# Prompt-key compression ahead of the state-space sums; stacking copies on ScalarE; low parts of K on VectorE

## The chip, the cores and the metric

The kernel runs on one core of one Trainium2 chip. TensorE (PE) multiplies, VectorE (DVE), ScalarE (ACT) and GpSimd (POOL) do the rest, and SyncE (SP) issues nearly all DMAs. The metric is device time in microseconds (us), as the median of several runs; a profile is one further execution, taken with the hardware profiler.

## The reference, cut to what matters

One layer of a hybrid decoder, for a prompt of 512 tokens and 8 single sample tokens (520 columns in all). A Mamba-2 branch and a sparse-attention branch read one normalised input; both are projected, merged and followed by a ConvFFN. The change touches the seam between the two branches:

```
y = _rmsnorm(y * silu(z), ssm_norm_w)            # end of the state-space branch
y_ssm @ w_ssm_out

def _compress(k, pe, w1, w2):                    # keys (and values) of the prompt, 32 tokens to one
    sub = k.reshape(b, nj, 16, N_KV_HEADS, 64)
    hid = einsum("ld,lde->e", pe, w1)
    for r in range(2):
        hid = hid + einsum("bjshd,sde->bjhe", sub, w1[r*16:(r+1)*16])[:, r:r+nc]
    return einsum("bnhe,ed->bnhd", silu(hid), w2)

scores = einsum("bqhgd,bkhd->bqhgk", q, k) * ATT_SCALE    # selected and window attention
```

The norm of the state-space branch needs the sum of squares over all 2048 channels of each token. The compression needs the first two K/V streams of all four KV heads. Attention of a head needs its K in two parts: a rounded high part and the low part, the rest, so that three cheap products stand for a float32 one.

## The kernel before, in words

Every weight matrix is read in tiles of 128x1024 floats (512 KB) by SP into one of two raw buffers, `wr`. ACT rounds each half to a high part `wh` (L310), and DVE or POOL subtracts it to give the low part `wl` (L315, in turn). A raw buffer is free for the next load when both of its halves are split. The weights w1k and w1v of the compression are used raw: their buffers are free only when TensorE has used them (`drop`). Loads are issued strictly in the order in which the program asks for the weights.

A dense tile (`dense`) is up to 8 steps of 6 matmuls into one of two PSUM buffers `d`; a third tile can start only when the first has been read out of its buffer.

`run` steps two generators, a main one and a side one. Each yields a cost; the side gets a step when the main's costs have paid for it. A planner (first pass) sets the ratio of the two. The instructions are then put in order, engine by engine, by a scheduler that works on this program order; each engine takes its instructions strictly in that order, and waits where one is not ready.

The stretch of the change is one such `run` in `emit`. Main: four tiles `cmp_tile(h)`, which project the keys and values of the compression, rotate the keys (`rope`: shuffle on DVE, product on POOL, product and sum on DVE), write them out, and stack even and odd tokens on two halves of the partitions by four copies into `KP` (named K in the profile, L1160 on DVE and L439 on ACT); then `y1(3)`, eight dense tiles of half length with the weights w_so, mixed with `pages`, 16 gathers by POOL (`P<-pool_kv`), each written back by SP (`dr_kv<-P`); then the projections of attention head 0. Side: `ssm_rstd`, which sums the squares (`s<-ones,SQ`), forms the reciprocal root and spreads it over the partitions (`s<-cst,V`); then `compress_p(0)`, 16 products with the stacked keys (`s<-K,wr`), a SiLU from a tanh on ACT, and products with w2k; then `compress_p(1)`, the same for the values. `ssm_rstd` begins by yielding RSA = 14000, so that it starts late, and has a second pause, RSC = 8000, before it spreads.

The attention heads are prepared in `head_in` (L1318 to L1328): ACT writes the high part of K twice, POOL and DVE subtract for one low part each, per branch.

Of the kernel before, what the change touches and what calls it, by code (L numbers as in the profile page):

```python
# [13 lines left out]
ALU = mybir.AluOpType  # L14
# [77 lines left out]
LEAD = 20  # L92
LEAD_B = 0
RSC = 8000.0
RSA = 14000.0
FC = 6
FLAG = 2
VLAG = 4
# [267 lines left out]
class Emit:  # L366
# [778 lines left out]
    def cmp_tile(self, h):  # L1145

        nc, pc = self.nc, self.pc
        d = yield from self.in_tile(("cmp", h))
        R = self.t(self.cp, "S2", [P, T], 4)
        self.act(R[64:128], d[64:128, OFF:OFF + T])  # L1150
        self.rope(d, 64, R)
        nc.sync.dma_start(self.A["o_kv"][3 * h], R)
        for j in range(2):
            src = R[64 * j:64 * j + 64, 0:SEQ].rearrange("p (n i s) -> p i n s", i=8, s=2)
            for s in range(2):
                dst = self.KP[64 * s:64 * s + 64, j, :, h, 0:32]
                if s == j:
                    self.act(dst, src[:, :, :, s])
                else:
                    nc.vector.tensor_copy(dst, src[:, :, :, s])  # L1160
        self.done.add(("cmp", h))

    def pages(self):
# [130 lines left out]
    def head_in(self, h):  # L1294

        nc, pc = self.nc, self.pc
        self.Q[h] = []
        for j in (2 * h, 2 * h + 1):
            d = yield from self.in_tile(("q", j))
            R = self.t(self.cp, "S2", [P, T], 4)  # L1300
            self.rope(d, P, R)
            for q in range(2):
                head = 2 * j + q
                Qs = self.t(pc, "Q", [P, SEQ], 8, F32R)
                a, b = slice(64 * q, 64 * q + 64), slice(64 * (1 - q), 64 * (1 - q) + 64)
                self.act(Qs[a], R[a, 0:SEQ], scale=0.125)
                self.stt(Qs[b], R[a, 0:SEQ], 0.125, Qs[a], ALU.mult, ALU.subtract)
                self.Q[h].append(Qs)
                hh = 64 * (h % 2)
                dst = self.qs[hh:hh + 64].rearrange("p a c x -> p (a c x)")  # L1310
                for par in range(2):
                    o = par * 256 + (h // 2) * P + par * 16 + head
                    self.ts(dst[:, o:o + 97:32], R[a, SEQ + par:T:2], 0.125, eng=nc.gpsimd)
        d = yield from self.in_tile(("k", h))
        R = self.t(self.cp, "S2", [P, T], 4)
        self.rope(d, P, R)
        nc.sync.dma_start(self.A["o_kv"][3 * h + 1], R)
        K = self.t(pc, "K", [P, 4, SEQ], 2, F32R)  # L1318
        self.K[h] = K
        for br in range(2):  # L1320
            a, b = slice(64 * br, 64 * br + 64), slice(64 * (1 - br), 64 * (1 - br) + 64)
            r = R[a, 0:SEQ]
            self.act(K[a, 2 * br], r)
            self.act(K[b, 2 * br], r)
            self.tt(K[a, 2 * br + 1], r, K[a, 2 * br], ALU.subtract, nc.gpsimd)
            self.tt(K[b, 2 * br + 1], r, K[a, 2 * br], ALU.subtract)
            hh = 64 * (h % 2)
            nc.gpsimd.tensor_copy(self.kn[hh:hh + 64, br, h // 2, :], R[a, SEQ:T])  # L1328
        d = yield from self.in_tile(("v", h))
        R = self.t(self.cp, "S2", [P, T], 4)  # L1330
        self.act(R, d[:, OFF:OFF + T])
        nc.sync.dma_start(self.A["o_kv"][3 * h + 2], R)
        yield 0.0
        pv = self.ps_s()
        for c in range(4):
            nc.tensor.transpose(pv[:, c * P:(c + 1) * P], R[:, c * P:(c + 1) * P], self.ident)
        V = self.t(pc, "V", [P, 4, P], 2)
        nc.vector.tensor_copy(V, pv.rearrange("p (c d) -> p c d", c=4))
        self.V[h] = V
        pn = self.ps_s()  # L1340
        nc.tensor.transpose(pn[0:NB, 0:P], R[:, SEQ:T], self.ident)
        nc.vector.tensor_copy(self.vn[:, :, h, :], pn[0:NB, 0:P].rearrange("p (a d) -> p a d", a=2))
        yield 500.0
        self.done.add(("head", h))
# [262 lines left out]
            self.act(self.G2[n], d[:, OFF:OFF + T], AF.Tanh, scale=0.5)  # L1607

    def ssm_rstd(self):
        yield RSA  # L1610
        for g in range(4):
            yield from self.need(("ssm", g))
        rb = []
        for part in range(2):
            lo, hi = self.span(part)
            d = self.ps_s()
            self.sums(d, self.SQ[:, lo:hi], True, True, part)
            rb.append(self.rstd5(d, 2048, self.pc, part, "V"))
        yield RSC
        self.rs = self.SQ  # L1620
        for part in range(2):
            lo, hi = self.span(part)
            self.act(self.rs[:, lo:hi], self.spread(rb[part], part))
        yield 1700.0
# [271 lines left out]
    def emit(self):  # L1896
        nc, tc, A = self.nc, self.tc, self.A
        self.X, self.BC, self.Z, self.Y, self.Q, self.K, self.V, self.F, self.HS = ({} for _ in range(9))

        def seq(*gens):  # L1900
            for g in gens:
                yield from g

        def ada(a, b):
            return seq(*[self.ada(nb) for nb in range(a, b)])
# [18 lines left out]
        with tc.tile_pool(name="cp", bufs=1) as self.cp, tc.tile_pool(name="ps", bufs=1, space=PSUM) as self.ps, \  # L1924
                tc.tile_pool(name="dr", bufs=1, space=DRAM) as self.dr:
            self.W = Weights(nc, self.cp, self.jobs(), self.order and self.order[1],
                             queue=lambda i: self.queue if i < 2 else nc.sync.dma_start)
            self.setup()
            self.phase_a()
            with tc.tile_pool(name="pb", bufs=1, reuse_waits="tile") as self.pb:  # L1930
                self.setup_b()
                self.done.add(("yfree", 0))

                def scan(g):
                    return mix(self.ssd(g), self.ssm_step(g))
                self.run(self.group_in(0), self.misc())
                self.run(seq(self.group_z(0), self.group_in(1)), scan(0), LEAD_B, PUSH)
                self.run(seq(self.group_z(1), self.y1(0), self.group_in(2)), scan(1), LEAD_B, PUSH)
                self.run(seq(self.group_z(2), self.y1(1), self.group_in(3)), scan(2), LEAD_B, PUSH)
                self.run(seq(self.group_z(3), self.y1(2)), scan(3), LEAD_B, 1.5)  # L1940
                nc.sync.dma_start(A["o_conv"], self.convo)
            with tc.tile_pool(name="mid2", bufs=1, reuse_waits="tile") as self.mid2:
                with tc.tile_pool(name="pc", bufs=1, reuse_waits="tile") as self.pc:
                    self.setup_c()
                    self.run(seq(*[self.cmp_tile(h) for h in range(4)], mix(self.y1(3), self.pages()), self.head_in(0)),
                             seq(self.ssm_rstd(), self.compress_p(0), self.compress_p(1)))
                    self.dump("Y1", self.Y1)
                    self.att_hi = self.t(self.cp, "S16", [P, KD, T], 4, F32R)
                    self.att_lo = self.t(self.mid2, "M16", [P, KD, T], 1, F32R)
                    for h in range(3):  # L1950
                        self.run(mix(seq(self.head_in(h + 1), self.gate1(range(2 * h, 2 * h + 2))),
                                     ada(8 + 3 * h, 11 + 3 * h)), self.attend(h), LEAD, PUSH_C)
                    self.run(mix(seq(self.gate1(range(6, 8)), self.gate2()), ada(17, 20)),
                             seq(self.attend(3), self.sample_attend()), LEAD, PUSH_C)
                    self.run(self.merge())
                with tc.tile_pool(name="pe", bufs=1, reuse_waits="tile") as self.pe:
                    self.W.extend(self.pe, 2, 1)
                    self.W.lo_engines = [nc.vector, nc.vector, nc.gpsimd]
                    self.x2 = self.t(self.pe, "x2", [P, KD, T])
                    nc.sync.dma_start(self.x2, A["xT"])  # L1960
                    self.run(self.out_proj())
                    self.dump("x2", self.x2)
                    with tc.tile_pool(name="pf", bufs=1, reuse_waits="tile") as self.pf:
                        self.setup_f()
                        for ci in range(len(F_CHUNKS)):
                            self.run(self.ffn_up(ci))
                            if ci == len(F_CHUNKS) - 1:
                                nc.sync.dma_start(A["o_ffn"], self.ffno)
                            self.run(self.ffn_down(ci))
# [30 lines left out]
```

## Time and profile before

| | us |
|---|---|
| median of 3 runs (lowest, highest) | 1459.07 (1458.52, 1460.3) |
| the profiled execution | 1463.65 |
| its span, first to last instruction | 1461.9 |

| engine | busy us | share of the span |
|---|---|---|
| PE | 1403.5 | 96% |
| DVE | 919.2 | 63% |
| ACT | 693.5 | 47% |
| POOL | 443.2 | 30% |

The busy time of PE is nearly the whole span, so that what the kernel can gain or lose is the time in which PE waits or runs at its lower clock. Times in the rows below are counted from the start of the span. In a timeline row the brackets hold the idle time just before the row's first instruction and what ended it.

### The profile page before, as it was taken

How to read it: one execution, taken by the hardware profiler on the slowest of the kernel's cores; microseconds unless marked ns; L12 is line 12 of the kernel's file. 1: busy time of each engine (PE TensorE's matmuls, PEld its weight loads, DVE VectorE, ACT ScalarE, POOL GpSimd, SP SyncE). 2: the span in 40 equal slices, each digit the busy share in tenths (PEclk: the TensorE clock that was granted, in tenths of full speed). 3: DMA queues.
4: the chain of work that ended last, by engine and by line, in shares of the span. 5: the costliest groups of instructions: out<-in, count | busy, mean ns of one | idle time of the engine just before them, and what ended most of it. 6: DMA issues, size and time to landing. Idle time of an engine off the chain costs nothing.

```text
span 1461.9 us, 28894 instructions
## 1 busy us (share of the span) xinstructions
PE 1403.5 (96%) x11407; PEld 1281.9 (88%) x11407; DVE 919.2 (63%) x1842; ACT 693.5 (47%) x1528; POOL 443.2 (30%) x466
## 2 busy tenths in 40 slices
PE   7999899999999899999999999999899999999996
PEld 5899698999898888887878787899799999999996
DVE  1678987688789657857577561244576636653653
ACT  2565656565664336636555462233454324432443
POOL 4113655355456644303122011121321111111114
PEclk8999999999999999999999999999999999999998
DMA  9646545355353574213131226326422234332221
GB/s 373 232 121 190 164 152 186 110 169 180 123 180 119 183 253 158 75 58 102 44 131 59 70 76 202 130 88 219 138 87 87 88 101 139 135 113 91 80 77 59
DMA packets 73672, 195.30 MB, mean 134 GB/s; under 512 B 8480, under 2 KB 21312, under 8 KB 73280
## 3 DMA queue, kind: packets, MB, share of 16 engines
q1 hardware_dynamic: 70272, 184.00, 38.1%
q0 software_dynamic: 2720, 8.92, 1.8%
q8 instruction: 90, 1.47, 0.4%
q10 hardware_dynamic: 544, 0.54, 0.1%
q14 instruction: 46, 0.38, 0.1%
HBM read 173.10 MB, written 24.49 MB: 135 GB/s over the span
## 4 chain that ended last, share of the span: by engine, by line
PE 79%; DVE 7%; DMA 6%; ACT 3%; issue 2%; POOL 2%; SPq 0%; DVEq 0%; ACTq 0%; POOLq 0%
PE d L391 62%; PE s L391 14%; PE s L1418 2%; DMA wr<-w_in 2%; DMA wr<-w_out 1%; ACT wh L310 1%; DVE wl L315 1%; DVE S L423 1%; DVE st L426 1%; POOL yd L423 1%; DMA S<-ada 1%; ACT S L439 1%; POOL sq L423 0%; POOL wl L315 0%; DMA csx<-dr_cs 0%
## 5 line engine op out<-in xcount | busy, mean ns | idle before, releaser
L391 PE MATMUL d<-S,wh 128*128 128x256 f32 (+1 forms) x4640 | 832.4, 290 | 27.1 <-DVE S L423 7.3
L391 PEld LDWEIGHTS d<-S,wh 128*128 128x128 f32 x4640 | 669.8, 191 | 56.2 <-issue 34.2
L391 PE MATMUL d<-S,wl 128*128 128x256 f32 (+1 forms) x2672 | 557.8, 286 | 1.0 <-DVE wl L315 1.0
L391 PEld LDWEIGHTS d<-S,wl 128*128 128x128 f32 x2672 | 422.8, 190 | 6.2 <-issue 4.5
L310 ACT ACTIVATE wh<-wr 128x512 fp32r<-128x512 f32 (+1 forms) x354 | 217.1, 622 | 386.4 <-PE d L391 305.9
L315 POOL TENSOR_TENSOR wl<-wr,wh 128x512 fp32r<-128x512 f32 (+1 forms) x147 | 196.3, 1336 | 611.4 <-ACT wh L310 556.9
L315 DVE TENSOR_TENSOR wl<-wr,wh 128x512 fp32r<-128x512 f32 x207 | 155.4, 753 | 122.7 <-ACT wh L310 110.6
L391 PE MATMUL d<-M,wh 128*128 128x256 f32 (+1 forms) x960 | 197.1, 284 | 0.9 <-DVE M L423 0.7
L391 PEld LDWEIGHTS d<-M,wh 128*128 128x128 f32 x960 | 149.7, 188 | 1.5 <-DVE M L423 0.9
L439 ACT ACTIVATE P<-s,sm 128x256 f32<-128x256 f32 (+3 forms) x128 | 66.7, 524 | 65.1 <-DVE sm L1400 61.0
L1400 DVE TENSOR_REDUCE sm<-s 128x1 f32<-128x512 f32 (+3 forms) x96 | 57.1, 596 | 33.0 <-PE s L391 32.3
L426 DVE SCALAR_TENSOR_TENSOR S<-d,fww,S 128x511 f32<-128x511 f32 x84 | 62.9, 749 | 14.4 <-ACT S L439 14.4
L439 ACT ACTIVATE PT<-s 128x512 f32<-128x512 f32 (+2 forms) x96 | 49.8, 523 | 39.8 <-PE s L1418 39.7
L439 ACT ACTIVATE S<-S 128x520 f32<-128x520 f32 (+4 forms) x83 | 49.3, 598 | 40.5 <-DVE S L423 16.9
L423 DVE TENSOR_TENSOR S<-S,S 128x520 f32<-128x520 f32 (+2 forms) x66 | 45.1, 683 | 35.5 <-ACT S L439 33.9
L391 PE MATMUL s<-PT,V 128*64 128x128 f32 x640 | 64.3, 286 | 0.0
L391 PE MATMUL s<-K,Q 128*128 128x256 f32 (+3 forms) x256 | 60.2, 337 | 1.8 <-ACT PT L439 1.6
L431 DVE TENSOR_SCALAR P<-P,sm,gates 128x256 f32<-128x256 f32 (+3 forms) x128 | 59.9, 489 | 2.4
L439 ACT ACTIVATE so<-bcb,xd 128x128 f32<-128x128 f32 x128 | 41.0, 391 | 40.9 <-DVE ys L1105 27.6
L426 DVE SCALAR_TENSOR_TENSOR st<-st,dts,so 128x128 f32<-128x128 f32 x128 | 54.1, 469 | 7.0 <-ACT so L439 7.0
L426 DVE SCALAR_TENSOR_TENSOR S<-d,cwh,S 128x511 f32<-128x511 f32 (+2 forms) x72 | 53.4, 741 | 1.2 <-ACT S L439 0.8
L426 DVE SCALAR_TENSOR_TENSOR x<-d,mod,x 128x512 f32<-128x512 f32 (+1 forms) x26 | 18.4, 710 | 55.2 <-PE d L391 55.1
(311 smaller groups left out, 1700.1 us busy)
## 6 DMA issues: line engine op xcount, KB each, us to landing
wr<-w_in SPq DMA_DIRECT2D x77, 512.0 KB
wr<-w_up SPq DMA_DIRECT2D x44, 512.0 KB
wr<-ada SPq DMA_DIRECT2D x40, 512.0 KB
st<-sst SPq DMA_DIRECT2D x32, 256.0 KB
csb<-dr_cs SPq DMA_DIRECT2D x16, 512.0 KB
o_ssms<-st SPq DMA_DIRECT2D x32, 256.0 KB
wr<-w_so SPq DMA_DIRECT2D x16, 512.0 KB
wr<-w_dn SPq DMA_DIRECT2D x16, 512.0 KB
```

The costliest lines, as they stand in the source:

```text
L310: r = self.nc.scalar.activation(hi[:, :n], raw[:, k0:k1], AF.Copy)
L315: eng.tensor_tensor(out=lo[:, :n], in0=raw[:, k0:k1], in1=hi[:, :n], op=ALU.subtract)
L391: r = self.nc.tensor.matmul(out, lhsT=l, rhs=r, start=start, stop=stop)
L423: return (eng or self.nc.vector).tensor_tensor(out=out, in0=a, in1=b, op=op)
L426: return self.nc.vector.scalar_tensor_tensor(out=out, in0=a, scalar=s, in1=b, op0=op0, op1=op1)
L431: return (eng or self.nc.vector).tensor_scalar(out=out, in0=a, scalar1=s1, scalar2=s2, op0=op0, op1=op1)
L439: return self.nc.scalar.activation(out, a, func, scale=scale, **kw)
L1400: nc.vector.tensor_reduce(sm[:, 0], ps, AX.X, ALU.max, negate=True)
L1418: nc.tensor.transpose(ps[:, i * n + k * P:i * n + (k + 1) * P], pr[:, i, k * P:(k + 1) * P], self.ident)
```

## The change

Three edits. In `emit` the side stream now begins with `compress_p(0)`; `ssm_rstd` follows, without its first pause, and then `compress_p(1)`. In `cmp_tile` all four stacking copies of a head go to ACT (two of four did so before). In `head_in` both low parts of K go to DVE (one of two was on POOL).

```
-RSA = 14000.0
...
             for s in range(2):
                 dst = self.KP[64 * s:64 * s + 64, j, :, h, 0:32]
-                if s == j:
-                    self.act(dst, src[:, :, :, s])
-                else:
-                    nc.vector.tensor_copy(dst, src[:, :, :, s])
+                self.act(dst, src[:, :, :, s])
...
-            self.tt(K[a, 2 * br + 1], r, K[a, 2 * br], ALU.subtract, nc.gpsimd)
+            self.tt(K[a, 2 * br + 1], r, K[a, 2 * br], ALU.subtract)
...
     def ssm_rstd(self):
-        yield RSA
         for g in range(4):
...
-                             seq(self.ssm_rstd(), self.compress_p(0), self.compress_p(1)))
+                             seq(self.compress_p(0), self.ssm_rstd(), self.compress_p(1)))
```

The order of instructions moves with it. On PE, in the stretch between the last `cmp_tile` and the first tiles of head 0, the 16 products with the stacked keys (`s<-K,wr`) stood in small groups between dense tiles (`d`), behind the sums of squares and their spreading (`s<-cst,V`). Before:

```order
L391 MATMUL s_6384<-cst_63,V_6185 128x8
L391 MATMUL s_6427<-K_5810,wr_6331 128x132
L391 MATMUL d_6337<-S_558_5591,wh_1_6327 128x256
...
L391 MATMUL s_6427<-K_5810,wr_6331 128x132 x7
L391 MATMUL d_6414<-S_558_5591,wh_1_6407 128x256
...
L391 MATMUL s_6427<-K_5810,wr_6466 128x132
```

and with the change (d_6231 is the second dense tile of `y1(3)`, d_6270 the third, d_6308 the fourth; SC and PT hold the SiLU's results):

```order
L390 MATMUL d_6231<-S_558_5591,wl_1_6117 128x264
L390 MATMUL s_6115<-K_5810,wr_6066 128x132 x8
L390 MATMUL s_6115<-K_5810,wr_6120 128x132 x8
L390 MATMUL s_6158<-SC_6150,sTn_5805 128x132
L390 MATMUL d_6270<-S_558_5591,wh_0_6142 128x256
L390 MATMUL d_6270<-S_558_5591,wh_0_6142 128x264
L390 MATMUL d_6270<-S_558_5591,wh_0_6142 128x256
L390 MATMUL d_6270<-S_558_5591,wh_0_6142 128x264
L390 MATMUL s_6159<-PT_5815,sTn_5805 128x512
L390 MATMUL s_6166<-ones_64,SQ_698 128x1 x2
```

All 16 now stand in one block behind the second tile of `y1(3)`, ahead of the third, and the sums of squares behind them.

On SP, the loads of the weights in the same stretch (w_so for `y1(3)`, w1k for the compression) among the writes of the pages (`dr_kv`). Before:

```order
L290 DMA wr_6066<-w_so 128x1024
L1152 DMA o_kv<-S_618_5954 128x520
L290 DMA wr_6143<-w_so 128x1024
...
L290 DMA wr_6254<-w_so 128x1024
L1152 DMA o_kv<-S_624_6096 128x520
L1169 DMA dr_kv_5823<-P_6115 128x512
L1169 DMA dr_kv_5823<-P_6124 128x512
L290 DMA wr_6331<-w1k 128x1024
```

and with the change:

```order
L289 DMA wr_6066<-w1k 128x1024
L1151 DMA o_kv<-S_618_5954 128x520
L289 DMA wr_6120<-w1k 128x1024
...
L1151 DMA o_kv<-S_624_6096 128x520
L1165 DMA dr_kv_5823<-P_6197 128x512
L1165 DMA dr_kv_5823<-P_6206 128x512
L289 DMA wr_6130<-w_so 128x1024
L1165 DMA dr_kv_5823<-P_6227 128x512
L1165 DMA dr_kv_5823<-P_6238 128x512
L289 DMA wr_6140<-w_so 128x1024
```

The two w1k loads have taken the places of the second and third w_so load, and these now stand where the w1k loads were, between the writes of the pages.

On ACT, from the stacking copies of the third head to the next high parts of weights. Before:

```order
L439 ACTIVATE K_5810<-S_621_6025 64x8x32
L439 ACT_TABLE_LOAD
L439 ACTIVATE rstd_6160<-rstd_6159 128x2
L310 ACTIVATE wh_1_6250<-wr_6066 128x512
L439 ACTIVATE K_5810<-S_621_6025 64x8x32
L310 ACTIVATE wh_0_6288<-wr_6143 128x512
L439 ACTIVATE S_624_6096<-d_6037 64x520
```

and with the change:

```order
L438 ACTIVATE K_5810<-S_621_6025 64x8x32 x4
L438 ACTIVATE S_624_6096<-d_6037 64x520
L438 ACTIVATE K_5810<-S_624_6096 64x8x32 x4
L438 ACTIVATE PC_6149<-s_6115,scm_6146 128x132
L438 ACTIVATE SC_6150<-s_6115,scm_6146 128x132
L438 ACTIVATE PT_6154<-PT_5815,scm_6146 128x512
L438 ACTIVATE PT_5815<-PT_5815,scm_6146 128x512
L309 ACTIVATE wh_0_6142<-wr_6130 128x512
```

The high part of the second w_so tile (wh_0_6142) now stands behind all stacking copies and behind the four operations of the compression's SiLU, which wait for the 16 products.

## Rows read from the trace of the kernel before

**Rows 1.** The page: busy time by engine (share of the span), x instructions
```profile
PE 1403.5 (96%) x11407; PEld 1281.9 (88%) x11407; DVE 919.2 (63%) x1842; ACT 693.5 (47%) x1528; POOL 443.2 (30%) x466
```
**Rows 2.** Busy time by stretch; its length; busy us (x instructions) of PE, PEld, DVE, ACT, POOL; clock; DMA
```profile
475.00:500.00 25.00, 20.18 (x153) 19.96 (x154) 20.41 (x42) 12.39 (x23) 17.76 (x22) 0.93 0.46 138
600.00:700.00 100.00, 98.46 (x803) 80.27 (x803) 69.97 (x148) 56.18 (x141) 24.91 (x28) 1.00 0.24 77
...
520.00:524.00 4.00, 4.00 (x24) 4.00 (x23) 1.45 (x3) 0.38 (x1) 1.98 (x3) 0.61 1.00 350
```
**Rows 3.** Timeline of PE; start, duration, what, [idle before, releaser]
```profile
489.20 0.28 PE L391 MATMUL s<-ones,SQ 128*128 128x1 f32 x2
491.88 0.72 PE L391 MATMUL d<-S,wh 128*128 128x256 f32 x4 [2.40 <-DVE rstd L423]
...
494.84 0.60 PE L391 MATMUL s<-cst,V 128*128 128x128 f32 x4
497.01 0.75 PE L391 MATMUL d<-S,wh 128*128 128x256 f32 x4 [1.56 <-DVE S L423]
...
515.32 1.74 PE L391 MATMUL s<-K,wr 128*128 128x132 f32 x14
519.56 0.72 PE L391 MATMUL d<-S,wh 128*128 128x256 f32 x4 [2.50 <-DVE S L423]
...
525.48 0.39 PE L391 MATMUL s<-K,wr 128*128 128x132 f32 x2
...
544.77 0.94 PE L391 MATMUL s<-K,wr 128*128 128x132 f32 x6 [0.89 <-DMA wr<-w1v]
```
**Rows 4.** Timeline of DVE
```profile
483.60 2.74 DVE L1160 COPY K<-S 64x256 f32<-64x256 f32 x4
...
487.05 0.74 DVE L1140 STREAM_SHUFFLE S<-d 64x520 f32<-64x520 f32 x1
...
491.05 0.68 DVE L423 TENSOR_TENSOR S<-d,S 64x520 f32<-64x520 f32 x1
...
493.60 0.74 DVE L1140 STREAM_SHUFFLE S<-d 64x520 f32<-64x520 f32 x1
...
514.75 4.05 DVE L423 TENSOR_TENSOR S<-S,SQ 128x520 f32<-128x520 f32 x5
```
**Rows 5.** Timeline of ACT
```profile
484.50 3.24 ACT L439 ACTIVATE K<-S 64x256 f32<-64x256 f32 x5
...
513.29 1.15 ACT L310 ACTIVATE wh<-wr 128x512 fp32r<-128x512 f32 x2 [9.83 <-DMA wr<-w_in]
...
530.77 1.28 ACT L439 ACT_TABLE_LOAD   x1 [6.00 <-DVE scm L430]
532.07 0.37 ACT L439 ACTIVATE PC<-s,scm 128x132 f32<-128x132 f32 x1
...
532.59 1.48 ACT L439 ACTIVATE PT<-PT,scm 128x512 f32<-128x512 f32 x2
```
**Rows 6.** Timeline of POOL
```profile
484.89 0.52 POOL L1194 MEMSET qs<- 128x512 f32 x1
...
494.42 1.29 POOL L423 TENSOR_TENSOR S<-S,rope 64x520 f32<-64x520 f32 x1 [3.31 <-DVE S L1140]
495.88 1.07 POOL L1208 DMA_INDIRECT P<-pool_kv,idx  x1 [0.17 <-issue]
```
**Rows 7.** Timeline of SP's queue of DMA issues
```profile
503.79 0.32 SPq L1169 DMA_DIRECT2D dr_kv<-P  x1
504.21 0.39 SPq L290 DMA_DIRECT2D wr<-w1k  x1
```
**Rows 8.** The chain of waits; start, duration; a DMA from its issue to its landing
```profile
508.55 4.64 DMA wr<-w_in
...
530.34 7.80 DMA wr<-w_in
...
541.10 3.63 DMA wr<-w1v
```
**Rows 9.** Instructions that write K; ns min/median/max
```profile
L423 DVE TENSOR_TENSOR K<-S,K x8: 686/1506/2326, 555.2 to 783.2; 64x512 fp32r<-64x512 f32 x8
L423 POOL TENSOR_TENSOR K<-S,K x8: 1262/1574/1778, 557.4 to 782.7; 64x512 fp32r<-64x512 f32 x8
```

## The prediction

> **What bounds the kernel now.** I read the busy times first: PE is busy for 96% of the span [rows 1], so a change is worth what it takes from, or adds to, the time in which PE stands still or runs at its lower clock. The second view is busy time by stretch. In the attention stretch from 600 to 700 PE is busy for 98.46 of 100 us; in the seam that the change rewrites, 475 to 500, for 20.18 of 25 [rows 2]. So there is nothing to win in the attention heads, and a few microseconds in the seam. The third view is the timeline of PE there. Four waits belong to what is moved: 2.40 us at 491.88, 1.56 at 497.01, 2.50 at 519.56 and 0.89 at 544.77 [rows 3], together 7.35. After the wait at 519.56 the granted clock is 0.61 of full speed from 520 to 524 [rows 2], that is 1.2 GHz for some 0.78 of that stretch and 2.4 GHz for the rest. From 519.56 to 525.48 PE did 36 matmuls in 5.92 us; at the pace of the 24 from 491.88 to 494.84 (2.96 us) they take 4.44 [rows 3]. A fall of the clock costs about 1.5 us here.
>
> **Low parts of K on DVE.** Eight instructions of 64x512 go from POOL to DVE. The row nearest to them is DVE's own: 0.69 us at best, 1.51 in the median and 2.33 at worst, while POOL's ran beside them in 1.26 to 1.78 [rows 9]. Alone on DVE, four in a row cost 2.8 us, where the pair with POOL beside it took 3.0 in the median. I cost this at nothing: PE's work on the scores of the head before hides it (98.46% busy). Without that cover it would be 8 x 0.69 = 5.5 us at most.
>
> **Stacking copies on ACT.** DVE loses eight copies; four of them alone took 2.74 us at 483.60 [rows 4]. ACT gets sixteen of 0.65 each (five in 3.24 [rows 5]). Starting no later than now, at 484.5, twelve end at 492.3; with one copy of the fourth tile's values (taken as long) and the last four, ACT is done at 495.5. PE wants the result at 495.8 (below), so they are just covered. If they were later, up to 2 us would still be hidden by the wait for the weights that follows.
>
> **The waits that go.** The wait of 2.40 is for a PSUM buffer: the rotated keys of the third tile are summed only at 491.05, since their shuffle began at 487.05, behind four copies, and more copies and the small operations of the root stood between [rows 4]. Now the shuffle comes at 483.6; POOL is free at 485.4, after its memset [rows 6], and multiplies in 1.29; with the sum of 0.68 the buffer is free at 487.4, before PE is through with the fourth tile at 489.2 [rows 3]. So 2.40 goes. The fourth tile's shuffle, at 493.60 now [rows 4], begins at 489.3, so POOL multiplies at 490.05 instead of 494.42: everything that hangs on it is 4.37 us earlier. The first tile of `y1(3)` runs from 489.2 to 492.15; its successor waits for one sum of 0.68, so of the 1.56 some 0.7 stays. It ends at 495.8. The wait of 2.50 was behind five multiplications by the root, 4.05 us on DVE from 514.75 [rows 4]. Six now stand in a row, but ahead of a sum that is wanted later, after another dense tile and eight products; I take 0.
>
> **What is late next.** The 16 products stand in one block. Their pace is (1.74 - 0.28) / 13 = 0.112 us a record (14 records at 515.32 [rows 3], the last one 0.28), two records each: 3.6 us, 495.8 to 499.4. Then PE has nothing that is ready. Next on its queue are the product with SC, which waits for the tanh, and the third dense tile of `y1(3)`, whose weights could not be loaded: both raw buffers held w1k until the eighth and the sixteenth product. On SP this load stands where w1k's stood, right behind the second write of a page, and that write waits for its gather. It was issued at 504.21, behind the write at 503.79 [rows 7], 8.3 us after the first gather began at 495.88 [rows 6]. With the gathers 4.37 earlier it is issued at 499.84, long after the eighth product (497.6). To its landing the chain shows 3.63, 4.64 and 7.80 for 512 KB [rows 8]; I take 4.64, the one with gathers and page writes beside it: 504.5. The high part is 0.58 (two in 1.15 [rows 5]), and PE goes on at 505.1. The wait is 5.7 us. From below: issued at the eighth product and landing in 3.63 it would be there at 501.2, but ACT comes to it only after the SiLU, from PC's start to PT's end 2.0 us [rows 5], with 0.4 ahead of it (estimate, two small DVE operations), so 502.4 and a wait of 3.0. From above: 7.80 makes 8.8.
>
> The Trainium skill, "DMA: Bandwidth & Descriptors", section "Anatomy of one DMA — SWDGE (gpsimd) path", fits a transfer by a fixed part of about 2.0 us and the bytes at 436 GB/s, there for the other path. By it 512 KB take 3.2 us (estimate), the wait would be 4.3 us and the sum about -0.95. All three rows of this stretch are above it, so the row stands.
>
> Two smaller ones. The root is now formed in one go, with a table load of 1.28 on ACT [rows 5] behind the next weights' high parts; by my count its spreading is ready 0.5 us after PE wants it (bounds 0 and 2). The first product with w1v stands behind the seventh tile of `y1(3)` and waits for a load of the same chain; I keep the 0.89 of now (bounds 0 and 4: a landing in 7.80 instead of 4.64).
>
> **The sum.** Before: 7.35. After: 0 + 0.7 + 5.7 + 0.5 + 0 + 0.9 = 7.8. The fall of the clock after the 2.50 goes; one after the 5.7 is taken in its place. So +0.45 us on the profiled execution's 1463.65, 1464.1. That is 0.03%; on the median of 1459.07, which is 0.3% below the profiled time, it gives **1459.5 us**.
>
> **Rivals.** *The block of products is cheap (faster).* The load lands soon after the eighth product, so that PE waits 3.0, and root and w1v cost nothing: 0.7 + 3.0 = 3.7, a gain of 3.65, or 1455.4; 1453.9 if the clock holds as well. For it: the waits of 2.40 and 2.50 go in any case, and the gathers are all started before the load. Against it: SP issues in order, and the page write behind the second gather came only at 503.79, some 7 us after that gather was issued [rows 6, 7].
>
> *The weight loads behind the pages' writes (slower).* One mechanism: with both raw buffers held by w1k, the loads of `y1(3)` come one after another through SP between page writes that wait for gathers, at a time when the DMA engines are full (share 1.00 from 520 to 524 [rows 2]). If each takes 7.80, the third tile waits 8.8 and the first w1v product some 3 more than now: 0.45 + 3.1 + 3 = +6.5, or 1465.6. It decides from where two loads of x us cost 0.45 + 2 (x - 4.64) = 2.9: x of 5.9. For it: 7.80 is a measured row. Against it: 3.63 and 4.64 are too, and the page writes of the gathers are spread out.
>
> *The change doesn't reach PE.* If the load were not on the path, because the scheduler's block of products were filled by ready tiles, the time would fall by all of 7.35 less 1.6, to 1453.3; the order on PE and SP speaks against it, and I give it little.
>
> **How the numbers follow.** A measurement of this kernel can tell about 0.2%, 2.9 us, from no change. The forecast (within 2.9 of 1459.1) has 0.48. Faster: 0.17 for the cheap block and 0.05 for a change that does not reach the load, 0.22. Slower: 0.30 for the loads. The forecast's own range, from the terms in the middle of their bounds, is 1457 to 1462; for 8 in 10 it has to reach into both others, to 1454 and 1466.
>
> **What would show it.** In the profile after: no wait of PE at the first tile of `y1(3)`; a wait below 1 us at its second; 16 products in 3.6 us without a gap at about 496 to 499; behind them one wait of 5 to 6 us, ended by ACT's high part or the DMA of w_so; a low granted clock in the microseconds after it; no wait of 2.5 for the multiplications by the root. In the heads PE as busy as now, with K's low parts on DVE at 0.69. I am wrong if the block waits for ACT's stacking copies, if the wait behind it is under 3 or over 9, or if PE loses time in the heads.

## The result, and the profile after

The changed kernel takes 1469.38 us, the median of six runs (1463.21 to 1473.68), against 1458.83 (1457.14 to 1463.07) for the kernel before on the same chip. The ratio worked out from all the runs is 1.0068, with a 95% interval of 1.0050 to 1.0087 (the two medians alone differ by 0.72%). The changed kernel is slower by some 10 us; the forecast was 1459.5, with a range of 1454 to 1466.

The two spans do not show it: 1461.9 us before, 1461.4 after. The run profiled of the changed kernel is the fastest of its six, and a stretch that the change does not touch differs by chance. From the output projection's first matmul to its first sum of squares (PE's timeline, before and after) it is 99.95 and 93.17 us:

```profile
947.35 0.40 PE L391 MATMUL d<-M,wh 128*128 128x256 f32 x2
...
1047.30 0.50 PE L391 MATMUL s<-ones,e 128*128 128x1 f32 x4
```
```profile
954.22 0.40 PE L390 MATMUL d<-M,wh 128*128 128x256 f32 x2
...
1047.39 0.50 PE L390 MATMUL s<-ones,e 128*128 128x1 f32 x4
```

In the twenty profiles of this study this stretch takes 93 to 102 us, in either order of the seam. So I compare one stretch instead of spans: from the last product of states (`s<-xdd,bt`) to the first transposition of head 0's values (`s<-cst,S`). It holds the same work in all kernels (714 or 715 matmul records). Called the seam below; the windows of PE (start:end, length, busy us, records, clock, DMA share, GB/s) are, for the kernel before, a second profile of it, the changed kernel, and a second profile of that:

```profile
459.09:557.66 98.57, 89.36 (x714) 0.97 0.60 192
```
```profile
459.36:558.58 99.22, 91.07 (x714) 0.95 0.60 195
```
```profile
459.88:566.54 106.66, 91.64 (x714) 0.95 0.55 182
```
```profile
451.05:558.77 107.72, 93.12 (x715) 0.92 0.55 179
```

The means are 98.9 and 107.2: 8.3 us, of which 6.1 are idle time (length less busy) and 2.2 busy time at a lower clock. The rest of the 10 us is within the interval. PE's timeline in the changed kernel, which answers to [rows 3]:

```profile
476.87 1.04 PE L390 MATMUL d<-S,wh 128*128 128x256 f32 x4 [2.32 <-DVE S L422]
...
495.50 0.74 PE L390 MATMUL d<-S,wh 128*128 128x256 f32 x4 [2.47 <-DVE S L422]
...
498.49 3.76 PE L390 MATMUL s<-K,wr 128*128 128x132 f32 x32
503.74 0.49 PE L390 MATMUL s<-SC,sTn 128*128 128x132 f32 x2 [1.49 <-DVE SC L425]
508.27 1.24 PE L390 MATMUL d<-S,wh 128*128 128x256 f32 x4 [4.03 <-ACT wh L309]
...
548.00 0.73 PE L390 MATMUL d<-S,wh 128*128 128x256 f32 x4 [2.08 <-DVE S L422]
...
558.13 1.90 PE L390 MATMUL s<-sTn,PT 128*128 128x64 f32 x16
...
566.54 0.66 PE L1332 MATMUL s<-cst,S 128*128 128x128 f32 x4 [2.51 <-ACT S L438]
```

The block and the wait behind it are there, 1.49 + 4.03 = 5.52 us; the wait of 2.50 for the multiplications is gone. The wait of 2.40 at the first tile of `y1(3)` is gone as well. But a wait of 2.47 stands ahead of the block, where 1.56 was, and two new ones, 2.08 and 2.51, stand at the end of the seam. The rows of DVE (the fourth tile's shuffle), ACT, POOL and SP [rows 4 to 7] show where the first comes from, and when the weights of the third tile are loaded:

```profile
493.53 0.01 DVE L1139 LOAD_MASK_SELECT S<-d  x1 [5.27 <-ACT S L438]
```
```profile
485.05 7.95 ACT L438 ACTIVATE K<-S 64x256 f32<-64x256 f32 x12
492.90 0.58 ACT L438 ACTIVATE S<-d 64x520 f32<-64x520 f32 x1
...
507.58 1.16 ACT L309 ACTIVATE wh<-wr 128x512 fp32r<-128x512 f32 x2 [2.86 <-DMA wr<-w_so]
...
543.37 1.15 ACT L309 ACTIVATE wh<-wr 128x512 fp32r<-128x512 f32 x2 [8.69 <-DMA wr<-w_in]
...
561.59 2.58 ACT L438 ACTIVATE K<-S 64x512 fp32r<-64x512 f32 x4 [3.50 <-DVE S L422]
564.08 1.52 ACT L438 ACTIVATE vc<-s 32x256 f32<-32x256 f32 x4
565.61 0.38 ACT L438 ACTIVATE vc_s<-s 128x256 f32<-128x256 f32 x1
565.89 0.60 ACT L438 ACTIVATE S<-d 128x520 f32<-128x520 f32 x1
```
```profile
495.77 1.07 POOL L1204 DMA_INDIRECT P<-pool_kv,idx  x1 [0.16 <-issue]
```
```profile
499.54 2.62 SPq L1165 DMA_DIRECT2D dr_kv<-P  x2
502.25 0.38 SPq L289 DMA_DIRECT2D wr<-w_so  x1
```

Twelve stacking copies on ACT end at 492.9, and only then comes ACT's copy of the fourth tile's values; the shuffle on DVE waits 5.27 us for it and begins at 493.53, where it began at 493.60 before. So the first gather is at 495.77, after 495.88 before, and not 4.37 us earlier. The load of w_so is issued at 502.25, right behind two page writes. The last four of ACT's rows are the end of the seam: the copy of head 0's values (565.89) stands behind K's copies and behind those of `vc` and `vc_s`. Before, the order on ACT was the other way round, and PE had the sixteen small products of the compression as its last work ahead of the transposition (PE, then ACT, of the kernel before):

```profile
555.43 1.89 PE L391 MATMUL s<-sTn,PT 128*128 128x64 f32 x16
557.66 0.66 PE L1336 MATMUL s<-cst,S 128*128 128x128 f32 x4 [0.34 <-ACT S L439]
```
```profile
557.03 0.58 ACT L439 ACTIVATE S<-d 128x520 f32<-128x520 f32 x1
557.51 1.51 ACT L439 ACTIVATE vc<-s 32x256 f32<-32x256 f32 x4
```

Now those products are at 558.13, in the middle of the dense tile of the values, and nothing covers the copy.

K's low parts (instructions that write K; ns min/median/max) take 686 ns in the median, where [rows 9] had 1506 with POOL's half beside them:

```profile
L422 DVE TENSOR_TENSOR K<-S,K x16: 683/686/1749, 562.3 to 791.0; 64x512 fp32r<-64x512 f32 x16
```

The Trainium skill ("SBUF — State Buffer", section "SBUF: two separate sides") calls the port pair of DVE and GpSimd an exclusive lock, where the loser waits for the whole instruction; the fall from 1506 to 686 agrees with it. The shorter instructions were worth nothing in time: PE is busy for 98.80 of the 100 us from 600, after 98.46 [rows 2].

### The profile page after: what moved, and what is told of

Read it like the earlier page. It is cut to its first block, busy times and chain, and to the rows that moved or that the text cites. A ratio compares the mean times of both kernels' runs of the same rounds, so it can differ in the third digit from the quotient of the medians.

```text
span 1461.4 us, 28891 instructions
## 1 busy us (share of the span) xinstructions
PE 1400.7 (96%) x11407; PEld 1279.9 (88%) x11407; DVE 909.8 (62%) x1842; ACT 698.0 (48%) x1536; POOL 431.9 (30%) x458
## 4 chain that ended last, share of the span: by engine, by line
PE 82%; DVE 6%; DMA 4%; ACT 3%; issue 3%; POOL 2%; SPq 0%; DVEq 0%; ACTq 0%; POOLq 0%
PE d L390 64%; PE s L390 14%; PE s L1414 2%; DMA P<-pool_kv,idx 1%; DMA wr<-w_in 1%; DVE st L425 1%; DMA dr_kv<-P 1%; ACT K L438 1%; DVE wl L314 1%; DVE S L422 1%; DMA S<-ada 1%; POOL wl L314 1%; POOL yd L422 0%; DVE S L425 0%; DVE yd L422 0%
## 5 line engine op out<-in xcount | busy, mean ns | idle before, releaser
L1414 PE MATMUL s<-cst,P 128*128 128x128 f32 x320 | 52.1, 276 | 1.6 <-DVE P L430 1.2
```

The source lines that it names most:

```text
L1414: nc.tensor.transpose(ps[:, i * n + k * P:i * n + (k + 1) * P], pr[:, i, k * P:(k + 1) * P], self.ident)
```

## The experiments

Each time is a ratio to the kernel before on the same chip, with its 95% interval. The lines of a diff are against the kernel before unless it is said; the diffs are cut to the lines that matter, and "..." marks what is left out.

**One edit at a time.** The third alone:

```diff
-        yield RSA
...
-   seq(self.ssm_rstd(), self.compress_p(0), self.compress_p(1)))
+   seq(self.compress_p(0), self.ssm_rstd(), self.compress_p(1)))
```

> Only the third edit: the compression of the prompt's keys ahead of the root of the state-space sums, without the 14000 of cost; the stacking copies split between ACT and DVE and K's low parts split between POOL and DVE as in the kernel before. Theory A (the order costs the time: 16 products with w1k stand in one block, both raw buffers stay full until its end, so the weights of y1(3) are issued late and PE waits behind the block and again before the values are transposed): +6 to +10 us over the kernel before, one wait of PE of 4 to 6 us behind the block. Theory B (the copies cost it: with all of them on ACT the copy of the fourth tile's values comes late, and with it the shuffle, the gathers and SP's queue): 1456 to 1460, and the wait behind the block under 3 us, since the fourth tile's shuffle then begins near 490.

Measured: 1.0066 (1.0044 to 1.0088), a seam of 106.70 us. PE and SP:

```profile
489.92 0.74 PE L390 MATMUL d<-S,wh 128*128 128x256 f32 x4 [1.23 <-DVE S L422]
...
492.91 3.76 PE L390 MATMUL s<-K,wr 128*128 128x132 f32 x32
498.16 0.49 PE L390 MATMUL s<-SC,sTn 128*128 128x132 f32 x2 [1.49 <-DVE SC L425]
504.30 1.24 PE L390 MATMUL d<-S,wh 128*128 128x256 f32 x4 [5.64 <-ACT wh L309]
```
```profile
492.59 5.29 SPq L1168 DMA_DIRECT2D dr_kv<-P  x2
497.97 0.38 SPq L289 DMA_DIRECT2D wr<-w_so  x1
```

The order alone costs as much as the whole change. With the copies split, the wait ahead of the block shrinks to 1.23, and PE waits the longer behind it, 7.13 instead of 5.52 (theory A had 4 to 6): the load of w_so is issued behind the second page write, which waits for its gather, 8.9 us after the first gather began (489.07), where it was 6.5 in the changed kernel.

The second alone, all stacking copies on ACT:

```diff
-                if s == j:
-                    self.act(dst, src[:, :, :, s])
-                else:
-                    nc.vector.tensor_copy(dst, src[:, :, :, s])
+                self.act(dst, src[:, :, :, s])
```

> Only the second edit: all sixteen stacking copies on ACT, the order and K's low parts as in the kernel before. Theory A: within 2 us of the kernel before, since the root stands ahead of the compression and nothing on PE hangs on the copies at once. Theory B: +4 to +8 us, with the fourth tile's shuffle on DVE waiting several us for ACT.

Measured: 1.0019 (1.0004 to 1.0035), a seam of 98.76 us. Theory B, which had 4 to 8 us, is not borne out; a cost of 0.6 to 5 us remains within the interval. In the seam the copies only move the waits: the one at the first tile of `y1(3)` is 4.23 where it was 2.40, and the others are shorter. The first edit alone:

```diff
-            self.tt(K[a, 2 * br + 1], r, K[a, 2 * br], ALU.subtract, nc.gpsimd)
+            self.tt(K[a, 2 * br + 1], r, K[a, 2 * br], ALU.subtract)
```

> Only the first edit: both low parts of K on DVE. Theories A and B: within 1.5 us of the kernel before, PE as busy in the heads as before (98.5 of 100 us). Rival C (the longer chain on DVE delays evictions in the heads): +2 to +5 us, and PE under 98 of 100 us from 600 to 700.

Measured: 0.9995 (0.9978 to 1.0012), with PE busy for 98.92 of 100 us from 600. Rival C falls. And the changed kernel once more:

> The changed kernel as it is, for a second profile. Theory A and theory B: about +10 us by the clock (1.0068 before), the seam from the third tile of the compression to the first transposed values of head 0 about 89 us in its profile, as in the first one, where the kernel before takes 82. Rival D (the loss varies from run to run and lies elsewhere, at the output projection or in the up and down projections): the seam near 82 to 84 and the loss behind 1000 us.

Measured: 1.0061 (1.0035 to 1.0088), a seam of 107.72 us. Rival D falls: the loss is in the seam in both profiles. The waits share it otherwise here, 1.50 + 4.74 = 6.24 us behind the block and 0.45 and 2.89 at the end:

```profile
499.92 1.23 PE L390 MATMUL d<-S,wh 128*128 128x256 f32 x4 [4.74 <-ACT wh L309]
```

The last profile of all is of the kernel before. Its seam, 99.22 us, lies just beyond the 97 to 99 expected, and far below the two of the changed kernel:

> The kernel before, for a second profile. If the seam is a property of the program, 97 to 99 us from the last state product to the first transposed values (98.6 in its first profile, 106.7 and 107.7 in the two of the changed kernel); if it varies from run to run, anything up to 105.

**The two halves of the third edit.** Without the pause alone, and the swap with the pause in front of both:

```diff
-        yield RSA
```

> Half of the third edit: the 14000 of cost is taken out, the root still stands ahead of the compression. The first eight products with w1k then stand one by one among the matmuls of y1(3), the second eight in a row. Theory A: no block of 16, but w1k holds a raw buffer longer: 0 to +4 us against the kernel before. Rival F (any start of the compression among the tiles of y1(3) costs the same, since it draws w1k ahead of w_so in the ring): +6 to +10 us.

```diff
+    def pause(self, us):
+        yield us
...
-   seq(self.ssm_rstd(), self.compress_p(0), self.compress_p(1)))
+   seq(self.pause(RSA), self.compress_p(0), self.ssm_rstd(), self.compress_p(1)))
```

> The other half: the compression ahead of the root as in the changed kernel, but the 14000 of cost kept in front of both; copies and K's low parts as before. The products then stand in small groups among the dense matmuls, with w_so prepared before them. Theory A: 0 to +3 us against the kernel before, no wait over 3 us behind the products. Rival F (it is the swap itself, the root behind the compression): +6 to +10 us.

Measured: 1.0030 (1.0014 to 1.0047) with a seam of 104.36 us without the pause, and 1.0016 (0.9998 to 1.0033) with 99.85 for the swap. The swap costs little, if anything, while the pause keeps the products among the dense matmuls. The early start does more: without the pause alone the seam is already 5.5 us longer than the mean before (98.9), of the 8.3 of the whole change, and PE waits 2.77 + 4.47 = 7.24 us behind the products although only eight of them stand in a row (PE; SP):

```profile
509.40 1.96 PE L390 MATMUL s<-K,wr 128*128 128x132 f32 x16
514.14 0.49 PE L390 MATMUL s<-SC,sTn 128*128 128x132 f32 x2 [2.77 <-DVE SC L425]
519.10 2.10 PE L390 MATMUL d<-S,wh 128*128 128x256 f32 x8 [4.47 <-ACT wh L309]
```
```profile
501.11 11.11 SPq L1168 DMA_DIRECT2D dr_kv<-P  x6
512.31 0.44 SPq L289 DMA_DIRECT2D wr<-w_so  x1
```

So a block of 16 is not needed for the wait: here too w_so is issued late, behind page writes. The full loss comes with both halves together.

**Own room for w1k.** Against the changed kernel:

```diff
+        self.w1k = self.t(pc, "K", [P, 2, 1024], 2)
+        for half in range(2):
+            nc.sync.dma_start(self.w1k[:, half], self.W.jobs["w1", 0, half][0])
...
-            w = self.W.get(("w1", j, half))
+            w = self.w1k[:, half] if j == 0 else self.W.get(("w1", j, half))
...
-            self.W.drop(("w1", j, half))
+            if j:
+                self.W.drop(("w1", j, half))
```

> The changed kernel, but w1k is loaded at the start of the stage into a free buffer of the tag K, and no longer through the two raw buffers of the weight ring; the 16 products still stand in one block. Theory A (both raw buffers held by w1k make the weights of y1(3) late; PE then waits 4.0 to 5.6 us behind the block and runs some 9.5 us at the lower clock): the wait behind the block falls under 1.5 us, the clock stays up, and the time is within 3 us of the kernel before (about -6 to -9 us against the changed one). Rival E (the block itself and the SiLU behind it cost the time, whatever the weights do): within 2 us of the changed kernel, +6 to +10.

Measured: 1.0040 (1.0020 to 1.0060), a seam of 101.83 us. The wait behind the block is gone, as theory A had it: the next dense tile follows at once. But the time is 6 us above the kernel before where theory A had at most 3: one wait has grown, to 5.28, and one is new, 2.95 (PE; ACT; DVE):

```profile
493.47 1.24 PE L390 MATMUL d<-S,wh 128*128 128x256 f32 x4 [5.28 <-DVE S L422]
...
499.50 3.77 PE L390 MATMUL s<-K,K 128*128 128x132 f32 x32
...
503.02 0.72 PE L390 MATMUL d<-S,wh 128*128 128x256 f32 x4
...
526.55 1.24 PE L390 MATMUL d<-S,wh 128*128 128x256 f32 x4 [2.95 <-DVE S L422]
```
```profile
481.73 6.64 ACT L438 ACTIVATE K<-S 64x256 f32<-64x256 f32 x10
...
490.21 0.63 ACT L309 ACTIVATE wh<-wr 128x512 fp32r<-128x512 f32 x1
```
```profile
490.87 0.69 DVE L314 TENSOR_TENSOR wl<-wr,wh 128x512 fp32r<-128x512 f32 x1 [6.26 <-ACT wh L309]
491.50 0.01 DVE L1139 LOAD_MASK_SELECT S<-d  x1
```

The fourth tile's shuffle now stands on DVE behind a low part of weights, whose high part stands on ACT behind the stacking copies. Four more kernels followed: the order alone with own room; the changed kernel with own room and copies issued one tile later; a version with the order, own room, K's low parts on DVE and later copies; and own room in the kernel before.

> The third edit (compression first, no pause) with w1k in its own buffer, the stacking copies split between ACT and DVE and K's low parts as in the kernel before. Theory A in two parts: (1) the ring's two raw buffers held by w1k cost what the order alone loses (1.0066); (2) what own room for w1k did not give back in the changed kernel is ACT's row of twelve stacking copies, behind which the high part of the next weights and with it DVE's queue and the fourth tile's shuffle stood (a wait of PE of 5.28 us). Then this kernel has no wait over 3 us ahead of the block, none over 1.5 behind it, and is within 2 us of the kernel before. Rival G (the loss of the order has a third part, in the tail: fewer products with w1v left to fill PE's gaps at head 0): +4 to +7 us, as with own room in the changed kernel.

> The changed kernel with w1k in its own buffer, and the stacking copies, still all on ACT, issued one tile later, in the middle of the next tile's rotation. Theory A, part 2: the fourth tile's shuffle no longer stands behind twelve copies, the wait of 5.28 us falls under 2.5, and the time is 2 to 6 us under the one with own room alone (1.0040), so within 3 us of the kernel before. Rival G: no gain over own room alone, +4 to +7 us.

> A version meant to beat both: compression first without the pause, w1k in its own buffer, both low parts of K on DVE, stacking copies split between ACT and DVE and issued one tile later. From the profile with own room alone (seam of 85 us from the third tile to the first transposed values) less the wait of 5.28 and its clock of about 1.2, the seam is 78 to 80 us against 81 to 82 in the kernel before: 1 to 3 us faster. Rival G: 2 to 5 us slower than the kernel before.

> The kernel before with w1k in its own buffer and nothing else: a control of what own room is worth without the block. Theory A: little, since w1k stands in the ring there only when y1(3) is nearly through: within 2 us of the kernel before. If own room gives as much here as it gave the changed kernel (4 us), it is no evidence on the block.

They took 1.0069 (1.0044 to 1.0094), 1.0046 (1.0026 to 1.0066), 1.0046 (1.0016 to 1.0076) and 1.0019 (0.9999 to 1.0040); the seams are 102.40, 104.63, 103.24 and 96.92. So theory A holds for the wait behind the block and not for the loss.

The copies one tile later, in the second and third of these, changed the program and not what the engines do: the order of the copies and shuffles on ACT and DVE in the seam is the same with and without them. In the second the shuffle still stands behind the low part that waits 6.26 us for ACT, and PE waits 5.26 us where it was to be under 2.5. That kernel is in effect the changed kernel with own room once more (1.0040), and the third is the order alone with own room plus K's low parts. Part 2 of theory A stays untested.

In the order alone with own room the next late weight makes the wait (PE; DVE), as it does in the two after it, with 4.18 and 5.89 us:

```profile
529.36 1.24 PE L390 MATMUL d<-S,wh 128*128 128x256 f32 x4 [2.72 <-DVE S L422]
```
```profile
528.01 0.69 DVE L314 TENSOR_TENSOR wl<-wr,wh 128x512 fp32r<-128x512 f32 x1 [7.97 <-ACT wh L309]
```

The copies one tile later were also tried in the kernel before. They are passed into the rotation, to stand between DVE's product and its sum (`last` holds the copies of the tile before):

```diff
-        self.rope(d, 64, R)
...
+        self.rope(d, 64, R, last)
```

> The kernel before with one edit of another kind: the stacking copies of a compression tile are issued in the middle of the next tile's rotation (between DVE's product and DVE's sum, while POOL multiplies), so that each shuffle comes first on DVE. If the wait of 2.40 us at the fourth tile is the price of copies ahead of the shuffle, it falls under 1 us, and the time by 1.5 to 3 us. If another wait of the seam (the sum of the first tile of y1(3), the DMA of w_so) takes it back: within 1 us of the kernel before.

Measured: 1.0003 (0.9983 to 1.0022). This says nothing on the theory either: DVE's four copies still begin at 483.85 and the third tile's shuffle at 487.31, after 483.60 and 487.05 before, and the wait at the first tile of `y1(3)` is 3.65, not under 1. The scheduler gives the engines the old order.

**Pages.** Theory H looked for the loss in the page writes on SP's queue. The pages spread, in the changed kernel, in the kernel before, and with the order and own room; and the writes alone issued two pages later:

```diff
-   mix(self.y1(3), self.pages()), self.head_in(0)
+   mix(seq(self.y1(3), self.head_in(0)), self.pages())
...
-            yield Aside(1000.0)
+            yield Aside(2500.0)
```

> The changed kernel with the sixteen page gathers and page writes spread over y1(3) and the first head's projections (2500 of cost each in place of 1000), so that fewer page writes stand ahead of each weight load on SP's queue and fewer transfers lie beside it. Theory H (the weights between the block and the values come late because their loads stand in SP's queue behind page writes that wait for gathers, and share the DMA engines with them; who holds the raw buffers matters little): 4 to 9 us less than the changed kernel (1.0061 to 1.0068), within 4 us of the kernel before. Theory G (the order itself leaves PE no filler: the products with w1k stand in one block and those with w1v are used up before the values): no gain, +7 to +11 us.

> The control: the same spreading of the pages in the kernel before. Theory H, if the pages are in the way of the changed order alone: within 2 us of the kernel before. If they cost this kernel as much (its waits for DMA of w1v and for the sums behind late weights): 2 to 5 us faster, and the spreading says little on the change.

> The order alone with w1k in its own buffer (1.0069 without the spreading) and the pages spread. Theory H: the weights of y1(3) and of the first head come in time, no wait of PE over 2 us between the block and the values, and the time is within 3 us of the kernel before. Theory G: +6 to +10 us.

> The changed kernel with each page's write issued two pages after its gather, the number and rate of gathers unchanged: what stands in SP's queue is the same, but a write seldom waits there for its gather. Theory H by the queue: 2 to 6 us less than the changed kernel. Theory H by the transfers (DMA engines shared) or theory G: within 2 us of the changed kernel, +8 to +11.

Measured, in this order: 1.0066 (1.0043 to 1.0089), 0.9984 (0.9968 to 1.0000), 1.0067 (1.0038 to 1.0095) and 1.0057 (1.0037 to 1.0076). The gain that theory H asked for is not there. The wait behind the block did shrink, to 1.49 + 2.15 us with the pages spread and 1.50 + 2.62 with the writes later, but the seams stayed at 106.46 and 108.14: the idle time of PE fell to 12.3 and 13.5 us (15.0 and 14.6 in the two profiles of the changed kernel), and its busy time rose to 94.2 and 94.6 (91.6 and 93.1), at a granted clock of 0.92.

Theory H is weakened by this and not excluded, because the edits moved little. Two page writes still stand ahead of the first load of w_so on SP, which is issued 6.0 and 6.2 us after the first gather (6.5 in the changed kernel), and with the pages spread eleven of the sixteen gathers still start before 520, as in the changed kernel. A kernel with the loads of w_so ahead of the page writes was not run.

A last version joined what had not cost anything in the old order (K's low parts on DVE, later copies, pages spread). As the later copies change nothing on the engines, it is the other two together:

> A second version meant to beat both, without the new order: the kernel before with both low parts of K on DVE, the stacking copies issued one tile later, and the pages spread over y1(3) and the first head's projections. If the gains of the single edits (0.9995, 1.0003 and 0.9984 of the kernel before) add up: 0.15 to 0.3% faster, 2 to 4.5 us, with 95 to 97 us from the last state product to the first transposed values (98.6 in the kernel before). If they take the same wait: no more than 2.5 us faster.

Measured: 1.0003 (0.9985 to 1.0021), a seam of 99.27 us. The gains don't add up, and the 0.9984 of the spread pages is not repeated; no version here is shown to beat the kernel before.

## Why the prediction was wrong

By its own steps, on the first pair of profiles, whose seams differ by 8.09 us:

- *K's low parts at nothing*: right, 0.9995 alone.
- *The copies on ACT just covered, the 2.40 gone, 0.7 of the 1.56 left*: the 2.40 did go, but 2.47 is left in place of 0.7, 1.8 too much. The step counted ACT's twelve copies and then one copy of the fourth tile's values, and never asked who waits for that one copy: the shuffle, and with it the gathers. The rows make it little more than a displaced cost, though: with the copies split the wait was 1.23, and the one behind the block grew by more; the copies alone took 1.0019.
- *The block of 3.6 us and 5.7 behind it*: 3.76 and 5.52, and the mechanism is the one named: w_so was issued right behind a page write, and the wait vanished with own room. That the size came out so well is in part luck. The block began 2.7 us late (498.49 for 495.8), w_so was issued 2.4 us late (502.25 for 499.84), and its high part began 5.3 us after that (507.58), where 4.64 was taken for the landing; these errors largely cancel. In the second profile the wait is 6.24. Nor does the reason for 4.64 hold: the load that took 7.80, from 530.34, had page writes beside it too, at 534.32.
- *The 2.50 gone, the root at 0.5, w1v at 0.9*: 0, 0 and 0, better by 1.4.
- *One fall of the clock in place of another*: right behind the block in this profile, by luck, and too cheap in general. The granted clock is 0.81 in the 7.73 us behind the block's wait, which is (1 - 0.81) x 7.73 = 1.5 us, as forecast. In the second profile of the same kernel it is 0.51 for 9.48 us, some 4.6, and in the order alone 0.53 for 9.70 (1.2 GHz for nearly all of it), some 4.6. Over the seam, busy time grew by 2.3 in this pair where 0 was taken. Most of that lies in a fall to which the prediction gave nothing, behind the new wait of 2.08 at the end: 0.66 for 5.00 us, some 1.7. The windows are those behind the block (changed kernel, all engines; its second profile and the order alone, PE) and behind the wait of 2.08 (changed kernel, PE):

```profile
508.27:516.00 7.73, 7.73 (x48) 6.70 (x49) 4.87 (x14) 4.12 (x9) 5.79 (x6) 0.81 0.90 274
```
```profile
499.92:509.40 9.48, 9.48 (x39) 0.51 0.88 278
```
```profile
504.30:514.00 9.70, 9.70 (x41) 0.53 0.82 290
```
```profile
548.00:553.00 5.00, 5.00 (x29) 0.66 0.14 53
```

- *The sum ended with the first product of w1v*: this is the step that failed most. The seam goes on to the values of head 0, and there the change adds 2.08 + 2.51 less the 0.34 of before, 4.25 us, and the 1.7 of lower clock just named, to which the prediction gave nothing. The two waits differ in kind. The one of 2.51, for ACT's copy of the values, stands in all five profiles with the new order and w1k in the raw buffers (1.9 to 2.9), where the eight with the old order have 0.5 or less. The rows of ACT and PE show the order behind it: the compression of the values is through earlier, so its small products no longer cover the wait for ACT's copy, and its copies stand ahead of it on ACT. No run changed this order alone. The one of 2.08 is one more late weight: a rotation stands on DVE behind a low part, whose high part waits 8.69 us on ACT for a load of w_in (543.37). It is not the same in every run; in the second profile it is 0.45. 0.8 more came ahead of the third tile of the compression (2.32 after 1.53).

Added up: 0.45 forecast + 1.8 - 0.2 - 1.4 + 4.25 + 0.8 + 2.3 = 8.0, of 8.09 measured. The rival named for a slower kernel, late weight loads behind page writes, gave 1465.6 and was nearest in time. Its mechanism is seen at the first load of w_so, but its two costs are not: the third tile of `y1(3)` waits 5.52 and not 8.8, and the first product with w1v not at all. That it came near is luck.

What stays open: the third edit is shown to be the one that costs the time, and w1k in the raw buffers to be what makes the wait behind the block, which goes with own room. With own room the seam is still 3 to 6 us longer than before. The rows show the waits moved on to the next late weight and to the values; no run here removed all of them at once, so it is argued and not shown that the order, with less side work left to fill PE later, is the cause of the rest. Own room in the order alone took 1.0069 (six runs) though its seam is 4.3 us shorter than without; its near twin with K's low parts took 1.0046, so part of this may be noise. Another part, 1 to 2 us, lies outside the seam: from the first sum of squares behind the output projection to the end the six kernels with own room take 415.0 to 416.4 us in their profiles, the fourteen others 413.9 to 414.9. Why is not shown.

## What to carry to other kernels

Side work that fills gaps is worth most where the main stream waits at its end, so moving it forward must be priced at the place that it leaves, not only where it arrives: follow the seam until both orders have done the same work. Waits in a chain of weight loads do not add up as separate terms; removing one shows the next, so what is late next must be asked once more than seems needed. When spans of single profiles vary by more than the effect, compare a stretch with the same instructions. And where a scheduler stands between the program and the engines, look in the trace whether an edit has changed the order there before its time is taken for or against a theory.

## What the runs showed of the hardware

Waits of the same kind had different prices, also in one kernel. After 5.52 us in which PE had only the product with SC the granted clock was 0.81 for 7.73 us, so that the lower clock cost about 1.5 us. After 6.24 us in the second profile of the same program it was 0.51 for 9.48, and after 7.13 us in the order alone 0.53 for 9.70, about 4.6 in each. The length of the wait alone does not set the price: without the pause, after 7.24 us, it was 0.72 for 6.90 (from 519.10 to 526.00), about 1.9. And DVE's subtraction of 64x512 fell from 1506 to 686 ns in the median once POOL no longer did the other half (686 too with that edit alone), so that DVE took over POOL's eight at no loss: sixteen at 686 are 11.0 us, eight at 1506 were 12.0.
